# The pooling branch's sixteen evictions: half on VectorE, half on ScalarE, or all on ScalarE

## Chip, cores and metric

The kernel runs on one core of one Trainium2 chip. The metric is the time of one execution in microseconds (us), the median of the timed runs of the same program. A core has a matrix engine (TensorE, PE in the rows, with its weight loads as PEld), a vector engine (VectorE, DVE), an activation engine (ScalarE, ACT), GpSimd (POOL), and queues that start DMA transfers (SP's and POOL's among them). Each engine works through its own list of instructions in order and waits at semaphores for the others. Matmuls write to PSUM, which is read out ("evicted") by VectorE or ScalarE.

## What is computed

One decoder layer, in float32, for 512 prompt tokens and 8 x 4 sample tokens (T = 544 columns in all). Three token mixers run on the same input and are merged by gates, and a feed-forward part follows:

```
h      = x @ w_in
gates  = sigmoid(h[..., o3:] + b_gate)                  # three branches
p      = pool_branch(u_a)                               # windows 2/4/8/16, 4 groups of 64 channels
br_a   = einsum('btgc,gcd->btgd', p, pool_w) * pool_scale
br_b   = stick_breaking_attention(q, k, v) @ w_att_o
glu    = c_in[..., :256] * sigmoid(c_in[..., 256:])
br_c   = silu(layernorm(causal_depthwise_conv31(glu))) @ conv_pw
merged = gates[0] * br_a + gates[1] * br_b + gates[2] * br_c
x      = layernorm(ALPHA * x + merged @ w_out)
x      = layernorm(ALPHA * x + (silu(x @ wg) * (x @ wu)) @ wd)
```

The change lies in the line of `br_a`: the product of the pooled input `p` with `pool_w`, times `pool_scale`.

## The kernel before

Activations are held with channels on the 128 partitions and tokens along the columns, in two halves (`HALVES`): 288 columns (32 sample and 256 prompt tokens) and 256. Every large product is done in float32 from parts: an operand is split into a rounded high part and the rest (`split_psum`, lines 213 to 219, and `_Weights.prepare`, line 120, with a cast on ScalarE at line 134 and a difference on VectorE at line 135), and `gemm` (line 221) issues three matmuls for each pair of operands (line 229). A chunk of 128 output columns over the 1024 inputs is 24 matmuls for each half; its result lies in one of three PSUM banks (pool `mm`).

Around the change the program says, in this order: the pooling input (lines 354 to 387, ending in `ph_` and `pl_`, the two parts of `p`), the convolution's inputs (390 to 408), the pooling branch's product (503 to 518), two gates of the first branch (`gate0`, 522), and then the attention with its q, k and v chunks (`qkv_q`, `qkv_k`, `qkv_v`). The depthwise convolution's 31 taps for each of two channel blocks (`conv_work`, line 437, 60 instructions on VectorE after the first of each) are handed out late in the program (`pump`), but depend on early data alone.

The order that each engine gets is not the program's. The framework's planner runs a timeline of its own, takes the instructions that are ready, goes by their place in the program, and writes a fixed list for each engine. A tile from a pool with one buffer is handed out again when all readers of the one before are done, and a pool that is closed gives its memory to pools opened later, whose tiles wait for the old readers (`reuse_waits="tile"`).

The pooling product is eight blocks (two group pairs `gp`, two column tiles `m`, two halves). A block takes `pair()`, a tile `z` of two banks from a pool with one buffer, and fills both banks: two groups of 64 channels, one for each half of the array's rows, three matmuls each (line 512). Its two banks are multiplied by `pool_scale` on the way out to `mg`: bank 0 on ScalarE (line 518), bank 1 on VectorE (line 516). The same tile `z` is next used by the attention's first scores (`front`, line 582). The pools `s1` and `pp` (which holds `ph_` and `pl_`) are closed behind the blocks (519, 520); the attention's pool `att` is opened at line 612, and `qkv_q` copies its chunk out with line 218 on ScalarE (`qh`), line 219 on VectorE (`ql`), and line 535 on ScalarE (`qbd`). The gates' chunks are copied out at line 491 on ScalarE, passed through a sigmoid (494), and multiplied into `mg` on VectorE (500). The convolution's result is transposed at line 458.

Of the kernel before, what the change touches and what calls it, by code (L numbers as in the profile page):

```python
# [13 lines left out]
ALU = mybir.AluOpType  # L14
# [33 lines left out]
V_BG, V_PS, V_CB, V_CG, V_CLB, V_G1, V_B1, V_DW, V_SB, V_SR = 0, 24, 32, 34, 36, 38, 46, 54, 116, 124  # L48
# [101 lines left out]
def hybrid_layer_kernel(  # L150
# [6 lines left out]
    nc = tc.nc  # L157
# [13 lines left out]
    def bank(tag="mm"):  # L171
        return pst[tag].tile([P, 512], F32, tag=tag, name=tag)
# [4 lines left out]
    def pair():  # L177
        return pst["z"].tile([P, 2, 512], F32, tag="z", name="z")
# [58 lines left out]
    def vcol(c):  # L237
        return vt[:, c:c + 1]
# [15 lines left out]
    mg = mp_.tile([P, KD, T], F32, name="mg")  # L254
# [249 lines left out]
    for gp in range(2):  # L504
        for m in range(2):
            for hf, (c0, c1) in enumerate(HALVES):
                zz = pair()
                pss = [zz[:, s] for s in range(2)]
                for n_, (a, b) in enumerate(((pw[0], ph_), (pw[0], pl_), (pw[1], ph_))):
                    for s in range(2):  # L510
                        r = slice(64 * s, 64 * s + 64)
                        nc.tensor.matmul(pss[s][:, :c1 - c0], a[r, gp, m * P:(m + 1) * P], b[r, gp, c0:c1], start=n_ == 0, stop=n_ == 2)
                for s in range(2):
                    mo = 4 * gp + 2 * s + m
                    if s:
                        nc.vector.tensor_scalar(mg[:, mo, c0:c1], pss[s][:, :c1 - c0], vcol(V_PS + mo), None, op0=ALU.mult)  # L516
                    else:
                        nc.scalar.mul(mg[:, mo, c0:c1], pss[s][:, :c1 - c0], vcol(V_PS + mo))
    s1s.close()
    pps.close()  # L520
    late_constants()
# [205 lines left out]
    for b in range(DB):  # L727
# [11 lines left out]
        for br, g in [c for c, n_ in zip(steps, at_batch) if n_ == b]:  # L739
# [3 lines left out]
            elif br == 3:  # L743
                cw_ = w.next()
                for m in range(2):
                    mo = 2 * g + m
# [38 lines left out]
    for g in range(4):  # L785
# [7 lines left out]
        for m, hf in both:  # L793
                mo = 2 * g + m
                c0, c1 = HALVES[hf]
# [340 lines left out]
    for m in range(KD):  # L1136
        pss = [bank(), bank()]
# [52 lines left out]
    for m in range(KD - 1):  # L1190
        pss = [bank(), bank()]
# [140 lines left out]
```

## Time and profile before

| | us |
|---|---|
| median of three timed runs | 854.65 |
| lowest and highest of them | 854.51, 855.94 |
| the profiled execution | 858.24 |
| its span, first to last instruction | 854.5 |
| TensorE busy | 824.3 (96%) |
| VectorE busy | 570.0 (67%) |
| ScalarE busy | 409.8 (48%) |
| GpSimd busy | 175.8 (21%) |

The page gives busy times over the whole span; what one stretch is limited by is read from the windows of that stretch and from what TensorE waited for there. Starts of instructions are in us from the span's start. "mm" is a bank of the pool of that name, "z" the pair of banks, "mg" the branch's result, "acc" the convolution's sum, "wh" and "wl" the two parts of a weight chunk.

### The profile page before, as it was taken

The numbers are of one execution on the slowest core, as the hardware profiler recorded it, in microseconds if no ns is written. First come the engines' busy times: TensorE is split into PE (matmuls) and PEld (weight loads), VectorE is DVE, ScalarE is ACT, GpSimd is POOL, SyncE is SP. The second block draws the span as 40 slices with busy tenths as digits, with TensorE's granted clock in tenths as the row PEclk, the third lists the DMA queues.
The fourth block names the chain that finished last, engine by engine and source line by source line (L and its number), as shares of the span: only waits on it lengthen the run. The fifth ranks groups of instructions, "written<-read, shape, count | busy, mean of one in ns | idle before, by whom it ended". The sixth has DMA issues, their size and how long they took to land.

```text
span 854.5 us, 16236 instructions
## 1 busy us (share of the span) xinstructions
PE 824.3 (96%) x6707; PEld 778.4 (91%) x6707; DVE 570.0 (67%) x956; ACT 409.8 (48%) x703; POOL 175.8 (21%) x200
## 2 busy tenths in 40 slices
PE   8999799999999999999999999999999999999992
PEld 7998799888798878789998999999999999999992
DVE  4899956889545545459645898873338988842436
ACT  5434368787635433334415665552214655543231
POOL 1430000001627787310000322111000211110002
PEclk9999899999999999999998999999999999999997
DMA  9413132422727989774710134312335333213222
GB/s 297 133 35 108 55 89 84 125 66 65 278 90 238 364 290 351 250 253 149 198 51 1 43 91 115 98 35 69 102 108 137 106 103 102 78 50 87 82 85 104
DMA packets 119401, 110.34 MB, mean 129 GB/s; under 512 B 4897, under 2 KB 111233, under 8 KB 117153
## 3 DMA queue, kind: packets, MB, share of 16 engines
q1 hardware_dynamic: 110848, 73.12, 28.8%
q0 software_dynamic: 8480, 36.20, 12.0%
q8 instruction: 52, 0.85, 0.4%
q14 instruction: 21, 0.16, 0.1%
HBM read 104.44 MB, written 4.87 MB: 128 GB/s over the span
## 4 chain that ended last, share of the span: by engine, by line
PE 87%; DVE 7%; issue 2%; DMA 2%; ACT 1%; POOL 1%; SPq 0%; DVEq 0%; ACTq 0%
PE mm L229 77%; DVE acc L437 3%; PE z L678 2%; PE o L705 2%; PE z L582 1%; PE o L608 1%; PE tp L603 1%; DVE wl L135 1%; PE tp L820 1%; DMA vr<-in_cv,piv 1%; DMA xt<-in_x_t 1%; PE tp L897 0%; DVE mg L516 0%; DVE mg L500 0%; POOL mg L751 0%
## 5 line engine op out<-in xcount | busy, mean ns | idle before, releaser
L229 PE MATMUL mm<-xh,wh 128*128 128x256 f32 (+1 forms) x672 | 198.6, 296 | 2.6 <-DVE gt L493 0.9
L229 PE MATMUL mm<-xl,wh 128*128 128x256 f32 (+1 forms) x672 | 196.8, 293 | 0.5 <-DVE xl L216 0.4
L229 PE MATMUL mm<-xh,wl 128*128 128x288 f32 (+1 forms) x672 | 196.2, 293 | 0.2 <-DVE wl L135 0.2
L134 ACT CAST wh<-raw 128x1024 fp32r<-128x1024 f32 (+2 forms) x93 | 84.8, 915 | 158.0 <-PE mm L229 140.4
L135 DVE TENSOR_TENSOR wl<-raw,wh 128x1024 fp32r<-128x1024 f32 (+2 forms) x93 | 99.3, 1070 | 66.9 <-ACT wh L134 66.3
L229 PEld LDWEIGHTS mm<-xh,wh 128*128 128x128 f32 x672 | 128.2, 191 | 8.7 <-issue 3.8
L229 PEld LDWEIGHTS mm<-xl,wh 128*128 128x128 f32 x672 | 128.1, 191 | 4.6 <-issue 3.1
L229 PEld LDWEIGHTS mm<-xh,wl 128*128 128x128 f32 x672 | 127.9, 191 | 3.0 <-issue 2.2
L229 PE MATMUL mm<-gh,wh 128*128 128x288 f32 (+1 forms) x352 | 101.5, 290 | 0.0
L229 PE MATMUL mm<-gh,wl 128*128 128x288 f32 (+1 forms) x352 | 101.1, 288 | 0.0
L229 PE MATMUL mm<-gl,wh 128*128 128x288 f32 (+1 forms) x352 | 100.7, 287 | 0.0
L645 POOL DMA_INDIRECT kr<-in_ck,pix x64 | 67.0, 1047 | 35.8 <-issue 15.4
L229 PEld LDWEIGHTS mm<-gl,wh 128*128 128x128 f32 x352 | 66.3, 188 | 0.0
L229 PEld LDWEIGHTS mm<-gh,wl 128*128 128x128 f32 x352 | 66.1, 188 | 0.0
L990 POOL TENSOR_TENSOR gl<-sg,gh 128x272 fp32r<-128x272 f32 x24 | 22.9, 956 | 209.5 <-ACT gh L989 209.5
L229 PEld LDWEIGHTS mm<-gh,wh 128*128 128x128 f32 x352 | 65.9, 188 | 0.1
L990 POOL TENSOR_TENSOR gl<-g,gh 128x272 fp32r<-128x272 f32 x20 | 21.3, 1066 | 110.2 <-ACT gh L989 107.8
L437 DVE SCALAR_TENSOR_TENSOR acc<-ge,vt,acc 128x512 f32<-128x512 f32 x60 | 42.5, 749 | 0.1
L229 PE MATMUL mm<-mh,wh 128*128 128x256 f32 (+1 forms) x128 | 37.7, 294 | 0.0
L229 PE MATMUL mm<-ml,wh 128*128 128x256 f32 (+1 forms) x128 | 37.5, 293 | 0.0
L229 PE MATMUL mm<-mh,wl 128*128 128x256 f32 (+1 forms) x128 | 37.0, 289 | 0.0
L914 DVE TENSOR_TENSOR wl<-rawf,wh 128x1024 fp32r<-128x1024 f32 x22 | 27.3, 1242 | 9.6 <-ACT wh L913 9.5
(327 smaller groups left out, 2158.4 us busy)
## 6 DMA issues: line engine op xcount, KB each, us to landing
raw<-in_w_in SPq DMA_DIRECT2D x14, 1024.0 KB, 6.3
rawf<-in_w_g SPq DMA_DIRECT2D x22, 512.0 KB, 4.0
rawf<-in_w_u SPq DMA_DIRECT2D x22, 512.0 KB, 5.4
raw<-in_w_in SPq DMA_DIRECT2D x12, 512.0 KB, 3.9
raw<-in_w_d SPq DMA_DIRECT2D x16, 384.0 KB, 3.5
raw<-in_w_d SPq DMA_DIRECT2D x16, 320.0 KB, 3.3
raw<-in_w_out SPq DMA_DIRECT2D x4, 1024.0 KB, 5.5
raw<-in_w_att_o SPq DMA_DIRECT2D x4, 512.0 KB, 3.5
```

The source lines that it names most:

```text
L134: self.nc.scalar.copy(hi[:, a:b], v[:, a:b])
L135: self.nc.vector.tensor_tensor(out=lo[:, a:b], in0=v[:, a:b], in1=hi[:, a:b].bitcast(F32), op=ALU.subtract)
L229: ins = nc.tensor.matmul(ps[:, :n], lw, rr, start=first and s == 0, stop=last and s == len(steps) - 1, **kw)
L437: nc.vector.scalar_tensor_tensor(out=o, in0=v, scalar=dw, in1=o, op0=ALU.mult, op1=ALU.add)
L582: nc.tensor.matmul(zps[s][:, :wd], a[r, qs], b[r, :wd], start=n_ == 0, stop=n_ == 2)
L603: nc.tensor.transpose(tp[:, kb], rc[:, s, kb * P:(kb + 1) * P], ident)
L608: nc.tensor.matmul(op_[64 * s:64 * s + 64, :P], vtok[:, kb, 64 * s:64 * s + 64], ats[s][:, kb], start=kb == 0, stop=kb == i)
L645: nc.gpsimd.indirect_dma_start(out=kr[:, u].rearrange("p h c -> p (h c)"), out_offset=None, in_=ck, in_offset=bass.IndirectOffsetOnAxis(ap ...
L678: behind["z"] = nc.tensor.matmul(zp[32 * jj:32 * jj + 32, :256], qbd[:, hp, b], kvt[b, "k", jj][:, :, hp], start=hp == 0, stop=hp == 3)
L705: nc.tensor.matmul(op_[32 * c:32 * c + 32], at[:, j], kvt[b, "v", j // 4][:, j % 4], start=j >= 4, stop=False)
L914: nc.vector.tensor_tensor(out=l, in0=src, in1=h.bitcast(F32), op=ALU.subtract)
L990: nc.gpsimd.tensor_tensor(out=gl[:, f % NFC, c0:c0 + TH], in0=g, in1=gh[:, f % NFC, c0:c0 + TH].bitcast(F32), op=ALU.subtract)
```

## The change

The choice between the two engines goes away: both banks of a block are now evicted by ScalarE, one after the other, with the operation that it used for bank 0. Data, order in the program and matmuls are the same.

```
                 for s in range(2):
                     mo = 4 * gp + 2 * s + m
-                    if s:
-                        nc.vector.tensor_scalar(mg[:, mo, c0:c1], pss[s][:, :c1 - c0], vcol(V_PS + mo), None, op0=ALU.mult)
-                    else:
-                        nc.scalar.mul(mg[:, mo, c0:c1], pss[s][:, :c1 - c0], vcol(V_PS + mo))
+                    nc.scalar.mul(mg[:, mo, c0:c1], pss[s][:, :c1 - c0], vcol(V_PS + mo))
```

## Rows read from the trace of the kernel before

**Rows 1.** Windows: length, busy us by engine, granted clock, DMA share, GB/s.

```profile
45.00:84.00 39.00, 37.95 (x304) 35.85 (x302) 38.96 (x56) 15.85 (x24) 6.00 (x7) 1.00 0.25 72
84.00:91.00 7.00, 1.46 (x15) 1.05 (x14) 7.00 (x13) 2.73 (x6) 0.00 (x0) 0.82 0.26 75
91.00:96.00 5.00, 4.81 (x25) 4.62 (x26) 5.00 (x9) 0.78 (x3) 0.21 (x1) 0.56 0.00 0
103.00:123.00 20.00, 20.00 (x162) 19.43 (x162) 11.05 (x20) 12.68 (x26) 1.32 (x2) 1.00 0.33 97
234.00:239.00 5.00, 4.06 (x23) 3.87 (x20) 2.68 (x7) 0.67 (x2) 0.00 (x0) 0.66 0.38 151
```

**Rows 2.** Instructions of line 512: duration min/median/max in ns, first and last start.

```profile
L512 PE MATMUL z<-ph,wh x16: 381/390/398, 45.1 to 85.9; 64*128 64x288 f32 x8, 64*128 64x256 f32 x8
```

**Rows 3.** Timeline, ScalarE: start us, duration us, operation, [idle before <- releaser].

```profile
80.80 1.06 ACT L134 CAST wh<-raw 128x1024 fp32r<-128x1024 f32 x1 [2.38 <-PE mm L229]
84.68 0.50 ACT L518 ACTIVATE mg<-z,vt 128x288 f32<-128x288 f32 x1 [2.82 <-PE z L512]
86.41 1.04 ACT L134 CAST wh<-raw 128x1024 fp32r<-128x1024 f32 x1 [1.23 <-PE z L512]
87.37 0.47 ACT L518 ACTIVATE mg<-z,vt 128x256 f32<-128x256 f32 x1
87.73 0.65 ACT L218 ACTIVATE qh<-mm 128x256 fp32r<-128x256 f32 x2
...
91.02 0.40 ACT L535 ACTIVATE qbd<-mm 64x32 f32<-64x32 f32 x2 [2.38 <-DVE ql L219]
```

**Rows 4.** Timeline, VectorE, same columns.

```profile
85.31 0.50 DVE L516 TENSOR_SCALAR mg<-z,vt 128x288 f32<-128x288 f32 x1
85.74 2.72 DVE L437 SCALAR_TENSOR_TENSOR acc<-ge,vt,acc 128x512 f32<-128x512 f32 x4
...
90.19 0.47 DVE L516 TENSOR_SCALAR mg<-z,vt 128x256 f32<-128x256 f32 x1
90.58 0.40 DVE L219 SCALAR_TENSOR_TENSOR ql<-mm,qh 128x256 fp32r<-128x256 f32 x1
```

**Rows 5.** Timeline, TensorE, same columns.

```profile
77.92 0.28 PE L229 MATMUL mm<-xh,wh 128*128 128x256 f32 x1
...
84.35 0.29 PE L512 MATMUL z<-ph,wl 64*128 64x288 f32 x2
85.87 0.39 PE L512 MATMUL z<-ph,wh 64*128 64x256 f32 x2 [1.23 <-DVE mg L516]
...
90.80 0.47 PE L582 MATMUL z<-kh,qh 64*128 64x128 f32 x2 [4.31 <-DVE mg L516]
91.47 0.58 PE L229 MATMUL mm<-xh,wh 128*128 128x256 f32 x1 [0.19 <-ACT qbd L535]
...
95.43 0.28 PE L229 MATMUL mm<-xh,wh 128*128 128x256 f32 x1
95.55 0.28 PE L229 MATMUL mm<-xl,wh 128*128 128x256 f32 x1
```

**Rows 6.** Groups by line, 40:112: xcount | busy us, mean ns | idle before.

```profile
L516 DVE TENSOR_SCALAR mg<-z,vt 128x288 f32<-128x288 f32 (+1 forms) x8 | 3.9, 485 | 0.0
L518 ACT ACTIVATE mg<-z,vt 128x288 f32<-128x288 f32 (+1 forms) x8 | 3.9, 485 | 2.8 <-PE z L512 2.8
```

**Rows 7.** TensorE's waits, 40 to 112 us: total us, times, longest us.

```profile
PE z L512 <- DVE mg L516: 1.7, 2, 1.2
PE mm L229 <- ACT gt L491: 0.6, 1, 0.6
```

**Rows 8.** Window of one us around 88 us, columns as in group 1.

```profile
88.00:89.00 1.00, 0.00 (x0) 0.00 (x0) 1.00 (x2) 0.64 (x3) 0.00 (x0) 0.77 0.00 0
```

**Rows 9.** Chain of waits around the convolution's first transposes: start us, us, what.

```profile
122.83 0.44 PE tp L458 x4
```

## The prediction, made before the change was run

> **What bounds the kernel now.** I read the windows by stage first, then TensorE's waits, then the rows of the four engines around the place where the change sits. TensorE is the bound: from 45 to 84 us it is busy 37.95 of 39 us, and from 103 to 123 us all 20 [rows 1]. The one early hole is 84 to 91 us: TensorE busy 1.46 of 7 us, VectorE busy all 7, and in 91 to 96 us the granted clock is 0.56 [rows 1]. So a change there is worth what of this hole it closes; VectorE's 8 evictions matter only as what TensorE waits for. In the 45 to 84 us window VectorE is busy 38.96 of 39 us and ScalarE 15.85 [rows 1].
>
> The hole comes about thus. The sixteen evictions belong to eight blocks of six matmuls (L512). All blocks go through one pair of banks, tile z, with one buffer: block n+1 cannot start before both evictions of block n are done. The blocks begin at 45.1 us and the last at 85.9 us [rows 2], (85.9 - 45.1)/7 = 5.8 us apart, though a block is only some 0.7 us of matmul. ScalarE's half of a pair is quick. VectorE's half stands in a full queue: for block 7 it begins 0.63 us after ScalarE's (85.31 against 84.68), for block 8 2.8 us after (90.19 against 87.37) [rows 3, 4]. In all eight pairs VectorE's begins later; 0.63 us is the smallest lag.
>
> The head pair's q columns follow. Their first half is finished in PSUM at 77.9 us [rows 5], ScalarE has 2.82 us idle before 84.68, yet it copies qh out only at 87.73, behind block 8's eviction [rows 3]. By the code that is a wait for memory: the pool att takes the space of ph and pl, which block 8 is the last to read. The trace shows the order, not the reason. With q and the first half of k unread, the three banks of mm are full, and TensorE stands: 1.23 us before block 8, then 4.31 us until VectorE's eviction at 90.19 frees z for the first scores (L582) [rows 4, 5].
>
> **The change part by part.** Removed from VectorE: eight L516, mean 485 ns alone [rows 6]; in a full queue the start of one to the start of the next instruction is 0.39 us (90.19 to 90.58) or 0.43 us (85.31 to 85.74) [rows 4], so 4 x 0.43 + 4 x 0.39 = 3.3 us. Alone, this moves VectorE's later work 3.3 us forward.
>
> Added to ScalarE: eight more L518, mean 485 ns, the same as VectorE's [rows 6]; behind another one the next starts 0.36 us later (87.37 to 87.73) [rows 3]. The second of a pair ends 0.36 us after the first, and 0.36 is under the smallest lag of 0.63 us. In sum 8 x 0.36 to 0.485 = 2.9 to 3.9 us on an engine with 23 of 39 us idle: I cost it at nothing, covered by that idle time; without that cover it is 3.9 us at most and never a gain. No wait of a new kind comes in. The second eviction waits for its block's last matmul, like the one ahead of it. Queued behind the pair are the weight casts (L134), the gate evictions (L491) and qh, and TensorE waits for the last two. A table load is not added, since the operation is that of the eight before. No DMA moves, and SP's and POOL's queues are not passed.
>
> One page speaks against the change. "TensorEngine Tiling (Array Packing)" of the Trainium skill, section "PSUM Bottleneck", says to use both ScalarE and VectorE for emptying PSUM. By that, a block's eviction would get 0.36 us longer; the rows say that it gets shorter in all eight, since VectorE is late by 0.63 us or more.
>
> What the hole is worth, by its own stretches:
> - 69 to 71 us: two waits, 0.5 us for L516 (1.7 less the 1.23) and 0.6 us for a gate's tile [rows 7], which waits for VectorE too: 1.1 us.
> - 84 to 91 us: 7 - 1.46 = 5.54 us [rows 1].
> - 91.47 to 95.43 us: 18 steps of matmul take 3.96 us, 0.22 us each, where the next takes 0.12 us (95.43 to 95.55) [rows 5]. That is the half clock, 1.2 GHz; it fell within 88 to 89 us (mean 0.77) after some 2 us without matmul [rows 8]. At the full 2.4 GHz, 18 x 0.117 = 2.1 us: 1.85 us to be had, and 0.2 us for the wait at 91.47.
>
> Sum 1.1 + 5.54 + 1.85 + 0.2 = 8.7 us. It is all to be had only if block 8 is through before q wants its memory at 77.9 us, so if a block takes no more than (77.9 - 45.1)/7 = 4.7 us in place of 5.8. A block's own time 0.7 us, two evictions 0.36 + 0.49, and a cast of 1.05 us in front of them (86.41, 1.04 us [rows 3]) make 2.6 us. The rest of a block's interval is where the planner puts it among the gate matmuls, which no row prices: between 0 and the 3.2 us that are left of today's 5.8. I take 2.0 us, since the planner can start a block from the moment z comes free, and so expect the last block to begin by 45.1 + 7 x 4.6 = 77.3 us or sooner.
>
> What is late next: VectorE's queue. If TensorE comes 8.7 us earlier and VectorE 3.3 us, VectorE trails by 5.4 us more than now. The taps need be done only for the first transposes of the convolution at 122.83 us [rows 9], and VectorE idles 20 - 11.05 = 8.95 us between 103 and 123 us [rows 1], so as a sum it fits. But ql (90.58 us, then qbd at 91.02 [rows 3, 4]) and the first scores stand in that queue, and each can make TensorE wait. Bounds: 0, if the idle time lies right, and the whole 5.4 us, if it does not. I take 2.2 us, nearest to the 1.23 us wait of block 8 with one more of its kind. Behind 123 us TensorE is nearly always busy, so an earlier TensorE carries through.
>
> Gain 8.7 - 2.2 = 6.5 us. The profiled execution took 858.24 us, 854.5 of it the span; the three timed runs have a median of 854.65 us. The gain is taken off either: 851.7 us for a profiled one, **848.2 us** for the median.
>
> **The rivals.**
> - The hole only shortens. The planner leaves the order of TensorE as it is, with blocks 7 and 8 behind k. Then block 7 is evicted at 84.68 + 0.36 + 0.50 = 85.54 in place of 85.81, block 8 ends 0.3 us earlier, the cast and two evictions run to 88.0, qh and kh to 89.1, and scores and second half of k come 1.8 us earlier; with the 1.1 us at 69 us that is 2.9 us, the clock still falling: 851.8 us. For: ScalarE's order around qh may stem from the planner and not from memory. Against: the planner places by when z is free.
> - VectorE is the bound. TensorE gains only what VectorE sheds, 3.3 us: 851.3 us. For: VectorE busy 38.96 of 39 us. Against: its idle time from 103 us on.
> - Given back later. The planner orders the rest anew, and a gap such as the one of 0.94 us that took the clock to a mean of 0.66 in 234 to 239 us [rows 1] (5 x 0.34 x 2 / 2 = 1.7 us) comes three or four times more: near 854.6 us, no change.
> - Slower. The taps that now run under the hole are put in front of ql, kl and the first scores, and three banks run dry three times as long as z did today for block 8: 3 x 3.7 us (86.5 to 90.19), with one more fall of the clock, 1.85 us: 13 us lost against 8.7 us won, 858.9 us. It decides once the new waits up to 123 us exceed 8.7 us. For: taps are always ready and fill VectorE. Against: the 8.95 us idle.
> - The page's rule, by a mechanism of this kernel: were VectorE prompt, serial evictions would hold z 0.36 us longer for eight blocks, 2.9 us: 857.5 us. The smallest lag of 0.63 us leaves it 2 in 100.
>
> **How the numbers follow.** Forecast 0.54 (its own range 846 to 851 us); hole shortened or VectorE the bound, 0.16 together; given back 0.13; slower by the taps 0.15; serial evictions 0.02. A measurement of this kernel tells some 0.2%, 1.7 us, from no change. Faster: 0.54 + 0.16 = 0.70; same 0.13; slower 0.15 + 0.02 = 0.17. The low end, 845 us, is the whole 8.7 us and part of one of the later falls of the clock; the high end, 856 us, takes in no change and the lesser losses. Left out: about 0.04 below and 0.12 above.
>
> **What would show it.** Right: no L516 on VectorE; the sixteen L518 in pairs 0.36 us apart; the last L512 before some 78 us; qh out right behind q's matmuls; no TensorE wait over 1 us and a granted clock of 1.00 from 84 to 96 us. Wrong: the last L512 still behind k's first half; TensorE waiting for ql, kl or zt behind taps; scores that begin earlier with convolution transposes no earlier; or a longer stretch behind 200 us.

## The result, and the profile after

The changed kernel takes 845.38 us (median of five runs, 843.94 to 849.24) beside 854.69 us (median of five) for the kernel before; the ratio is 0.9879, with a 95% interval of 0.9847 to 0.991. By the medians it is 9.3 us faster, by the ratio 10.3 us (7.7 to 13.1), where 6.5 us were forecast. Side by side it was run three times more, with ratios of 0.9906 (0.9874 to 0.9939), 0.9897 (0.9834 to 0.9961) and 0.9926 (0.9895 to 0.9956). In three of the five groups of runs below the kernel before took 874 to 880 us and not 855, and in the traces of these groups the excess lies behind 200 us; so a kernel's time is compared with that of the kernel before in its own group, and the stretch of the change by its own length.

The profiled execution took 845.32 us, its span 843.5 us. In the windows around the change (length, busy us of TensorE, its weight loads, VectorE, ScalarE, GpSimd, then granted clock) the hole of [rows 1] is gone:

```profile
45.00:84.00 39.00, 39.00 (x313) 36.62 (x312) 38.93 (x54) 21.52 (x37) 6.59 (x7) 1.00 0.29 85
84.00:91.00 7.00, 7.00 (x58) 6.83 (x57) 6.46 (x11) 2.56 (x7) 0.97 (x1) 1.00 0.03 7
91.00:96.00 5.00, 5.00 (x44) 4.92 (x44) 4.58 (x10) 3.06 (x8) 0.54 (x1) 1.00 0.51 161
84.00:123.00 39.00, 39.00 (x315) 37.55 (x316) 34.55 (x62) 23.12 (x49) 3.06 (x5) 1.00 0.29 84
```

TensorE is busy without a gap from 45 to 123 us, at a clock of 1.00. ScalarE's share of the first stretch went from 15.85 to 21.52 of 39 us; VectorE is still full there, with no eviction of the product in it. The instructions of the blocks and of the evictions (minimum, median and maximum in ns, first and last start; then count, busy us and mean ns) answer to [rows 2] and [rows 6]:

```profile
L512 PE MATMUL z<-ph,wh x16: 381/390/398, 45.7 to 75.8; 64*128 64x288 f32 x8, 64*128 64x256 f32 x8
```

```profile
L515 ACT ACTIVATE mg<-z,vt 128x288 f32<-128x288 f32 (+1 forms) x16 | 6.9, 486 | 3.7 <-PE z L512 3.6
```

The blocks are (75.8 - 45.7)/7 = 4.3 us apart in place of 5.8. The last one begins 3.3 us before q's first half is finished at 78.79 + 0.29 = 79.08 us, with this matmul:

```profile
78.79 0.29 PE L229 MATMUL mm<-xh,wl 128*128 128x288 f32 x1
```

Sixteen evictions on ScalarE take 486 ns each. ScalarE's and VectorE's timelines (start us, duration us, operation, idle before and releaser) answer to [rows 3, 4]:

```profile
77.35 0.84 ACT L515 ACTIVATE mg<-z,vt 128x256 f32<-128x256 f32 x2
78.07 1.12 ACT L494 ACTIVATE gt<-gt 128x1088 f32<-128x1088 f32 x1
79.21 1.28 ACT L293 ACT_TABLE_LOAD   x1
80.50 0.39 ACT L218 ACTIVATE qh<-mm 128x256 fp32r<-128x256 f32 x1
81.92 0.38 ACT L218 ACTIVATE qh<-mm 128x256 fp32r<-128x256 f32 x1 [1.03 <-PE mm L229]
```

```profile
82.80 0.73 DVE L219 SCALAR_TENSOR_TENSOR ql<-mm,qh 128x256 fp32r<-128x256 f32 x2
...
85.92 0.41 DVE L216 TENSOR_TENSOR kl<-mm,kh 128x256 fp32r<-128x256 f32 x1
```

Block 8's pair leaves at 77.35 us, and behind a sigmoid and a table load qh follows at 80.50, 7.2 us sooner than before; ql follows at 82.80. From 40 to 112 us the table of TensorE's waits is empty, where [rows 7] stood. The three longest waits of TensorE behind 112 us (total us, times, longest):

```profile
PE tp L894 <- DVE y L886: 1.5, 1, 1.5
PE mm L229 <- DVE gt L493: 0.9, 1, 0.9
PE o L605 <- ACT at L601: 0.7, 1, 0.7
```

To measure the stretch alone I take the time from the first block's first matmul to the first product of the new keys (line 663 before, 660 after), where both kernels have done the same work: 221.1 - 45.1 = 176.0 us before, 212.8 - 45.7 = 167.1 us after, **8.9 us less**.

```profile
L663 PE MATMUL z<-qbd,ksf x8: 379/379/403, 221.1 to 222.7; 128*32 128x256 f32 x8
```

```profile
L660 PE MATMUL z<-qbd,ksf x8: 379/379/403, 212.8 to 214.4; 128*32 128x256 f32 x8
```

The two profiled spans differ by 11.0 us. Behind the new keys the changed kernel takes another 2.7 us less (854.5 - 221.1 = 633.4 us against 843.5 - 212.8 = 630.7 us), and its first block begins 0.6 us later. The section on the prediction shows what of the 2.7 us is the clock.

### The profile page after: what moved, and what is told of

The parts are those of the page before. It is cut to its first block, busy times and chain, and to the rows that moved or that the text cites. A ratio compares the mean times of both kernels' runs of the same rounds, so it can differ in the third digit from the quotient of the medians.

```text
span 843.5 us, 16236 instructions
## 1 busy us (share of the span) xinstructions
PE 819.7 (97%) x6707; PEld 773.2 (92%) x6707; DVE 568.2 (67%) x948; ACT 413.2 (49%) x711; POOL 177.3 (21%) x200
## 4 chain that ended last, share of the span: by engine, by line
PE 93%; DMA 2%; DVE 2%; ACT 1%; issue 1%; POOL 1%; SPq 0%; DVEq 0%; POOLq 0%; ACTq 0%
PE mm L229 83%; PE z L675 2%; PE o L702 2%; PE z L579 1%; PE o L605 1%; PE tp L600 1%; PE tp L817 1%; DMA vr<-in_cv,piv 1%; DMA xt<-in_x_t 1%; PE z L512 1%; PE tp L894 0%; PE o L705 0%; POOL mg L748 0%; ACT xf L895 0%; POOL kr L642 0%
## 5 line engine op out<-in xcount | busy, mean ns | idle before, releaser
L135 DVE TENSOR_TENSOR wl<-raw,wh 128x1024 fp32r<-128x1024 f32 (+2 forms) x93 | 101.2, 1091 | 67.3 <-ACT wh L134 66.7
L229 PEld LDWEIGHTS mm<-xh,wh 128*128 128x128 f32 x672 | 126.5, 188 | 8.7 <-issue 4.0
L229 PEld LDWEIGHTS mm<-xl,wh 128*128 128x128 f32 x672 | 126.2, 188 | 4.5 <-issue 3.1
L229 PEld LDWEIGHTS mm<-xh,wl 128*128 128x128 f32 x672 | 126.2, 188 | 3.3 <-issue 2.4
```

Source lines behind the costliest of these rows:

```text
L135: self.nc.vector.tensor_tensor(out=lo[:, a:b], in0=v[:, a:b], in1=hi[:, a:b].bitcast(F32), op=ALU.subtract)
L229: ins = nc.tensor.matmul(ps[:, :n], lw, rr, start=first and s == 0, stop=last and s == len(steps) - 1, **kw)
```

## The experiments

Two theories were set against each other. The pace theory: the time is set by when z comes free; that places block 8 in TensorE's list before or behind q and k, and block 8 holds the memory that q's copies wait for. The relief theory: VectorE is full, and the gain is what it sheds. The table gives the stretch (first block to new keys) and the time against the kernel before in the same group. The kernel before has one trace. Two traces of the same program differ by up to 1.4 us in the stretch (e2 and e10), so a difference of 2 us there is not far from that.

| kernel | stretch, us | ratio (95%) |
|---|---|---|
| before | 176.0 | 1 |
| changed (e8, e15, e18) | 167.4, 167.1, 167.1 | 0.9906, 0.9897, 0.9926 |
| all sixteen on VectorE (e1, e9) | 174.1, 173.0 | 0.996 (0.9926 to 0.9994), 0.9969 (0.9947 to 0.9991) |
| blocks 1 to 4 on ScalarE (e2, e10) | 173.9, 172.5 | 0.9974 (0.9946 to 1.0002), 0.9956 (0.9925 to 0.9987) |
| blocks 5 to 8 on ScalarE (e3, e11) | 174.2, 173.8 | 0.9935 (0.9913 to 0.9956), 0.9929 (0.9901 to 0.9958) |
| changed, VectorE's load back (e4, e12) | 167.1, 167.1 | 0.9979 (0.9949 to 1.001), 0.9901 (0.9866 to 0.9935) |
| changed, three times that load (e13) | 173.9 | 1.0022 (0.9985 to 1.0059) |
| before, ph and pl in memory of their own (e5) | 169.3 | 0.992 (0.9889 to 0.9952) |
| changed, the same (e6) | 167.1 | 0.9889 (0.9844 to 0.9934) |
| before, taps held back (e7) | 185.8 | 1.0094 (1.0062 to 1.0127) |

The time follows the stretch to within 3 us, except in e3 and e11 (by the ratio 5.7 and 6.2 us faster, by the stretch 1.8 and 2.2), e4 (1.8 against 8.9) and e13 (1.9 us slower against 2.1 us faster). By the traced executions these differences lie outside the stretch, and no run here explains them; what follows is told by the stretch.

**All on one engine, the other one.**

```
-                    if s:
-                        nc.vector.tensor_scalar(mg[:, mo, c0:c1], ...)
-                    else:
-                        nc.scalar.mul(mg[:, mo, c0:c1], ...)
+                    nc.vector.tensor_scalar(mg[:, mo, c0:c1], ...)
```

> All sixteen evictions on VectorE, none on ScalarE. Pace theory (the time is set by when tile z comes free, and so where the planner puts block 8 in TensorE's list): z is freed by VectorE's queue as before, the list has block 8 behind the first half of k again, so the hole at 84 to 91 us stays and the pair's second half adds some 0.4 us to it: 855 to 856 us. Relief theory (the gain is the 3.3 us of work that VectorE sheds): VectorE gets 3.3 us more in a stretch where it is always busy: 858 us.

> All sixteen evictions on VectorE again, since the kernel before took 879 us on the chip of the first four and not 855. There the stretch of 84 to 96 us still had a hole (TensorE busy 7.71 of 12 us, clock 0.72). Pace theory: block 8 starts some 2 us earlier than in the kernel before and the hole shrinks but stays: 852 to 855 us. Relief theory: 3.3 us slower than before, 858 us.

Before e1 both theories expected the kernel before or worse; it was 2 to 3 us shorter in the stretch and 0.3 to 0.4% faster in time, and e9 repeated it. VectorE had some 3.3 us more to do, so a relief cannot be what made this gain. The hole stayed, smaller (TensorE busy 2.71 of 7 us in e9, before 1.46), and was now TensorE waiting for kh and for qbd (total us, times, longest):

```profile
PE mm L229 <- ACT qbd L532: 2.4, 1, 2.4
PE z L579 <- ACT kh L215: 1.8, 1, 1.8
```

**Half of the blocks.**

```
-                    if s:
+                    if s and gp == 1:        # e2, e10; gp == 0 in e3, e11
```

> Both evictions on ScalarE for blocks 1 to 4 only; blocks 5 to 8 split as before. Pace theory: blocks 2 to 5 come closer together, but block 8 still stands behind the first half of k in TensorE's list, so the hole at 84 to 91 us and its half clock stay and only the 1.1 us of waits near 70 us can go: 853 to 854.5 us. Relief theory: half of 3.3 us, with the measured gain shared evenly half of 9.3 us: 850 to 853 us.

> ScalarE alone for blocks 1 to 4, again. Pace theory: block 8 behind the first half of k, hole and half clock stay, 852 to 854.5 us. Relief theory: half the gain, 850 us.

> Both evictions on ScalarE for blocks 5 to 8 only; blocks 1 to 4 split as before. Pace theory: block 8 is still behind the first half of k in TensorE's list, but z is freed by ScalarE some 1.8 us sooner; the hole is shorter and the clock falls all the same or just escapes: 851 to 853 us. Relief theory: half, 850 to 853 us, with no difference from blocks 1 to 4.

> ScalarE alone for blocks 5 to 8, again. Pace theory: the hole is shorter by some 2 us and the clock falls all the same, 851 to 853 us. Relief theory: half the gain, 850 us, the same as for blocks 1 to 4.

Half of the blocks gave 1.8 to 3.5 us of the 8.9 in the stretch, whichever half it was. By the time alone e3 and e11 would fit the relief theory's half as well or better (5.7 and 6.2 us); it is the traces that tell the two theories apart here. In e10 block 8 stood behind the first half of k as before, began at 83.5 us, and TensorE waited for its eviction on VectorE with the clock falling again (the wait, then the windows as above):

```profile
PE z L582 <- DVE mg L516: 2.6, 1, 2.6
```

```profile
84.00:91.00 7.00, 3.36 (x17) 3.00 (x16) 7.00 (x13) 3.02 (x8) 0.21 (x1) 0.78 0.25 72
91.00:96.00 5.00, 5.00 (x40) 5.00 (x40) 5.00 (x8) 1.32 (x3) 0.00 (x0) 0.97 0.00 0
```

So the gain in the stretch is not shared out by blocks: the hole closes when block 8 is not left behind q and k, and 4.3 us a block do that while a mix does not (last blocks at 83.5 to 85.7 us). e3 and e11 are the rival "the hole only shortens" in the flesh: they keep the waits near 70 us, so its price is 1.8 us without the 1.1, and 1.8 and 2.2 us were measured in the stretch. That e10 won more than the 1.1 us of the waits near 70 us was not expected; its block 8 began at 83.5 us, before at 85.9.

**VectorE's load given back, once and three times.** To the changed kernel this adds instructions on VectorE that take the maximum of a piece of mg with itself; z is freed by ScalarE alone as before.

```
                     nc.scalar.mul(mg[:, mo, c0:c1], pss[s][:, :c1 - c0], vcol(V_PS + mo))
+                    if s:
+                        for _ in range(3):   # e13; once in e4, e12
+                            nc.vector.scalar_tensor_tensor(out=mg[:, mo, c0:c1], in0=mg[:, mo, c0:c1], scalar=1.0, in1=mg[:, mo, c0:c1], op0=ALU.mult, op1=ALU.max)
```

> The changed kernel with eight instructions added on VectorE (each takes the maximum of a piece of mg with itself, some 0.4 us), so that VectorE has its old load back while z is still freed by ScalarE alone. Pace theory: block 8 stays ahead of q in TensorE's list and the time stays that of the changed kernel, 845.4 us, within 1.5 us. Relief theory: the 3.3 us come back, 848.7 us or more.

> The changed kernel with eight instructions of some 0.4 us on VectorE, again. On the chip of the first four there was no hole from 45 to 123 us. Pace theory: 846 us within 2 us, or up to 2 us more if VectorE, which now trails by the whole 8.7 us, makes TensorE wait behind 123 us. Relief theory: 849 us or more, with waits for VectorE already between 84 and 123 us.

The added instructions (count, busy us, mean ns) and the windows in e12:

```profile
L517 DVE SCALAR_TENSOR_TENSOR mg<-mg 128x288 f32<-128x288 f32 (+1 forms) x8 | 3.4, 431 | 0.0
```

```profile
45.00:84.00 39.00, 39.00 (x313) 36.62 (x312) 38.93 (x59) 21.65 (x37) 6.91 (x7) 1.00 0.29 85
84.00:91.00 7.00, 7.00 (x58) 7.00 (x57) 6.63 (x11) 2.44 (x7) 0.97 (x1) 1.00 0.02 5
91.00:96.00 5.00, 5.00 (x44) 4.75 (x43) 4.58 (x11) 2.77 (x6) 0.54 (x1) 1.00 0.51 161
```

With 3.4 us of the shed work back on VectorE the stretch is 167.1 us in both runs, to the tenth the changed kernel's, and TensorE has no gap from 45 to 96 us. The relief theory falls for the stretch. In e12 the whole gain is there in the time too (0.9901); in e4, the same program, most of it was given back behind 200 us, where TensorE waited in many places (busy 113.82 of 130 us from 200 to 330 us, 117.79 in e12). As the two have one order, the order alone does not make that difference; its cause is open.

> The changed kernel with 24 such instructions on VectorE, three to a block, some 9 us of work in all. From its first block to the first product of the new keys the changed kernel takes 167.1 us, and with eight of them also 167.1 us; VectorE idles about 4.5 us between 84 and 123 us of the changed kernel. If VectorE has slack in this stage only by its idle time: 6 to 9 us more than it has are asked of it, TensorE waits for it and the stretch grows by 2 to 5 us. If the planner only moves the taps behind what TensorE needs, and the convolution's transposes go later with other work in front: 167 to 168 us still, and no new wait over 0.6 us before 123 us.

TensorE's waits from 100 to 213 us (total us, times, longest), and the window behind 123 us:

```profile
PE tp L603 <- ACT at L604: 1.8, 1, 1.8
PE tp L603 <- ACT cf L472: 0.8, 1, 0.8
PE z L582 <- DVE zt L584: 0.6, 1, 0.6
```

```profile
123.00:213.00 90.00, 86.72 (x691) 77.07 (x690) 71.40 (x138) 65.62 (x131) 8.38 (x14) 0.94 0.25 77
```

Three times the load, 9.9 us (9.0 of it from 45 to 84 us), made the stretch 6.8 us longer: TensorE now waited, not in the old place but behind 140 us, in the attention and behind the convolution's norm, 90 - 86.72 = 3.3 us in all, and the clock fell (a mean of 0.94 there, where the changed kernel has 1.00). Two of the three waits end with ScalarE's work; that VectorE's queue is behind them follows from the edit alone. So VectorE's slack in the stretch lies between the 3.4 us of e12, which cost nothing, and 9.9 us. Of the two expectations the first was nearer, with its 2 to 5 us too small.

**The memory.** ph and pl become parts of oh, which nothing writes before the attention's first output; the attention's pool then takes over no memory from them.

```
-    ph_ = pp.tile([P, 2, T], F32R, name="ph")
-    pl_ = pp.tile([P, 2, T], F32R, name="pl")
+    ph_, pl_ = oh[:, 0:2], oh[:, 2:4]
```

> The kernel before, split evictions as they were, but ph and pl lie in oh, which is not written until the attention's first output, in place of a pool whose memory the attention's tiles take over. Memory theory: q's copies no longer wait for block 8, so the banks of mm come free, TensorE goes on with q, k, v and gates while the blocks trickle through, and most of the 7.5 us around 84 to 96 us goes although z is as slow as before: 846 to 849 us. If the planner's order alone put qh behind block 8: no change, 854.7 us.

The blocks' matmuls with their first and last start, the windows, and ScalarE's first copy of q:

```profile
L511 PE MATMUL z<-oh,wh x32: 273/338/405, 46.8 to 91.9; 64*128 64x288 f32 x16, 64*128 64x256 f32 x16
```

```profile
84.00:91.00 7.00, 7.00 (x58) 6.67 (x57) 6.48 (x11) 2.68 (x6) 0.66 (x1) 1.00 0.27 77
91.00:96.00 5.00, 5.00 (x43) 4.70 (x42) 5.00 (x9) 1.98 (x4) 0.54 (x1) 1.00 0.10 28
```

```profile
80.02 0.38 ACT L218 ACTIVATE qh<-mm 128x256 fp32r<-128x256 f32 x1
```

Here VectorE evicts its half as before, and the last block's matmuls begin at 91.9 us, later than before; yet TensorE has no hole, since qh is copied out at 80.02 us, ahead of the last blocks. The stretch is 6.7 us shorter. What the trace of before showed as an order was a wait for memory. The change and this edit cure the same thing from its two ends, as the two together show:

> The changed kernel with ph and pl in oh. Memory theory: block 8 is through before q asks for the memory, so nothing is left to gain: 845.4 us, within 1.5 us. If memory still held something up in the changed kernel, 843 us or less.

167.1 us, and 0.9889: nothing is added. The 2.2 us between e5 and the changed kernel contain the two waits near 70 us, which e5 still has (TensorE 37.90 of 39 us from 45 to 84 us).

**The queue of taps.**

```
+                    with tc.issue_after(hold.ins):   # hold: the last eviction
-                    nc.vector.scalar_tensor_tensor(out=o, in0=v, scalar=dw, in1=o, op0=ALU.mult, op1=ALU.add)
+                        nc.vector.scalar_tensor_tensor(out=o, in0=v, scalar=dw, in1=o, op0=ALU.mult, op1=ALU.add)
...
-                        nc.vector.tensor_scalar(mg[:, mo, c0:c1], ...)
+                        hold = nc.vector.tensor_scalar(mg[:, mo, c0:c1], ...)
```

> The kernel before, split evictions, with the convolution's taps held back on VectorE behind its last eviction of the product, so that VectorE's half finds a short queue. If the queue of taps is what makes VectorE's half late: z comes free within 1 to 2 us of each block, block 8 is through well before 78 us, and the hole at 84 to 91 us is gone; 40 us of taps then start some 25 us later and the convolution's transposes with them, which TensorE may have to wait for: 846 to 851 us. If VectorE's half is late for another reason (the weight differences of 1.2 us, the order of the two engines): the hole stays and the late taps come on top, 856 us or more.

VectorE's evictions (line 517 there) and one of ScalarE's, then the windows, then TensorE's waits:

```profile
54.66 0.48 DVE L517 TENSOR_SCALAR mg<-z,vt 128x256 f32<-128x256 f32 x1 [1.55 <-ACT mg L519]
...
59.21 0.52 DVE L517 TENSOR_SCALAR mg<-z,vt 128x288 f32<-128x288 f32 x1 [1.85 <-ACT mg L519]
...
68.38 0.52 DVE L517 TENSOR_SCALAR mg<-z,vt 128x288 f32<-128x288 f32 x1 [2.37 <-ACT mg L519]
...
72.88 0.48 DVE L517 TENSOR_SCALAR mg<-z,vt 128x256 f32<-128x256 f32 x1 [1.25 <-ACT mg L519]
```

```profile
54.15 0.47 ACT L519 ACTIVATE mg<-z,vt 128x256 f32<-128x256 f32 x1 [2.04 <-PE z L513]
```

```profile
45.00:84.00 39.00, 39.00 (x316) 36.65 (x315) 17.43 (x25) 17.80 (x29) 5.55 (x8) 1.00 0.24 73
84.00:91.00 7.00, 6.95 (x54) 6.51 (x53) 7.00 (x13) 2.85 (x7) 0.00 (x0) 1.00 0.25 75
```

```profile
PE tp L472 <- DVE cna L466: 4.1, 1, 4.1
PE tp L459 <- DVE acc L438: 2.0, 2, 1.8
```

With the taps away VectorE is idle before four of its eight evictions and the hole is gone (6.95 of 7 us), so it was the queue of taps that made VectorE's half late enough to matter. That block 8 would be through well before 78 us did not come true: the blocks are 4.8 us apart (47.5 to 81.4 us), and the last begins 1.3 us behind the end of q's first half (79.78 + 0.29 us):

```profile
79.78 0.29 PE L229 MATMUL mm<-xh,wl 128*128 128x288 f32 x1
...
81.40 0.39 PE L513 MATMUL z<-ph,wh 64*128 64x256 f32 x2
```

So block 8 need not be ahead of q, as the prediction asked; a little behind it cost nothing. But 40 us of taps that start after 80 us are late for the convolution's transposes and norm (4.1 and 2.0 us of waits, and a clock of 0.91 from 123 to 213 us), and the kernel is 0.9% slower where 4 to 9 us faster was expected: the taps have to run in that stretch.

**The changed kernel again**, in each later group:

> The changed kernel again, beside the three above on the same chip: 845.4 us, with a spread of some 2 us between runs, as the clock falls or not after the short waits behind 200 us.

> The changed kernel beside the other two on the same chip: 167.1 us from the first block to the new keys, and 0.990 of the kernel before.

> The changed kernel beside the two, for the same chip: 0.990 of the kernel before.

It came out at 847.16, 871.18 and 849.16 us (beside 856.28, 879.66 and 855.02 us), with the stretch at 167.1 to 167.4 us each time.

**The same for the gates.** The evictions of line 493 move to ScalarE: 32 of them, of the second and third branch (not 36, as the first expectation says), and in e17 the last four as well.

```
-                if br == 0 and g < GACT:
+                if br or g < GACT:             # e14, e16; always in e17
```

> The changed kernel with the evictions of all other gates (line 493) moved from VectorE to ScalarE too, 36 of them. In the changed kernel TensorE waits 0.9 us for one of them near 225 us and once or twice 0.7 us beside it. If what held for the product's evictions holds here (the engine with the shorter queue frees the bank sooner): 0.5 to 1.5 us faster than the changed kernel, 844 to 846 us. If ScalarE, whose sigmoids, exponentials and table loads stand in the same queue there, frees the banks later: 1 to 4 us slower, 847 to 850 us.

> The changed kernel with the gates of the second and third branch evicted by ScalarE too (32 instructions of line 493; the four of the first branch's fourth gate stay on VectorE), again. On the last chip, where the kernel before took 879.7 us, it was 863.2 us beside 871.2 us for the changed kernel. On a chip where the kernel before takes 855 us the waits that it takes away are 0.9 us for a gate and some of 0.7 us: 843 to 845 us beside 846.

> The same with the four evictions of the first branch's fourth gate moved as well, so that no gate is evicted by VectorE. If every eviction moved to the shorter queue helps: the 0.3 us that TensorE still waited for line 493 goes, the time as with 32 or up to 0.5 us less. If the order planned anew decides: any difference within 2 us.

Each stands beside the changed kernel in its own group: e14 had 0.9828 (0.9773 to 0.9884) against 0.9897 (0.9834 to 0.9961), e16 and e17 had 0.9928 (0.9904 to 0.9951) and 0.9904 (0.9873 to 0.9935) against 0.9926 (0.9895 to 0.9956). The intervals overlap each time: no difference that these runs can tell. The wait for line 493 went from 0.9 us (e18) to 0.3 us in e16, and to none in e17, but the wait for page data grew from 0.4 us (e18) to 2.4 and 1.7 us (total us, times, longest, in e17):

```profile
PE o L702 <- DMA vr<-in_cv,piv: 1.7, 1, 1.7
```

So it is no sure improvement on the changed kernel.

## Why the prediction was right in kind and too small

- **What bounds it, and the hole.** Right. The memory that block 8 holds, told from the code alone, is now shown by e5, and VectorE's late half and its queue by e7. The three full banks and the fall of the clock were not tried by themselves; they went with the hole in e5, e7 and the changed kernel. That block 8 must be through before q is finished is stricter than e7 shows.
- **The worth of the hole, 8.7 us.** Right: the stretch got 8.9 us shorter.
- **The block's interval.** At most 4.6 us was forecast, 4.3 us came; the last block at 75.8 us where 77.3 or sooner was forecast.
- **ScalarE at nothing.** Right: 5.7 us more busy time from 45 to 84 us and no wait of TensorE for it before 112 us.
- **New waits for VectorE, 2.2 us.** This is the step that failed: they were 0. I took them from the wait of block 8, though that wait came of VectorE's late half of z, which the change removes. The rows had the answer: the idle 8.95 us from 103 to 123 us cover the 5.4 us by which VectorE trails. From 84 to 123 us VectorE idled 39 - 29.53 = 9.47 us before and 39 - 34.55 = 4.45 us after, so 5.0 us were taken up there:

```profile
84.00:123.00 39.00, 33.27 (x256) 31.82 (x255) 29.53 (x50) 18.96 (x39) 2.07 (x4) 0.91 0.28 83
```

  That TensorE did not wait for ql and kl on the way is measured; that the planner sees to it by putting them ahead of taps is argued, not shown. e13 shows that the worry was real: with 9.9 us of further work waits do come, and the stretch is 6.8 us longer. Without the 2.2 us the forecast would have been 854.65 - 8.7 = 845.95 us.
- **What lies behind 200 us.** The ratio of 0.9879 is 10.3 us of 854.69 us, so 844.4 us, just below the low end of 845 us, where the forecast had the whole 8.7 us and a part of one later fall of the clock. What the stretch leaves of it is 1.4 us. The falls differ between executions of one program: at the last norm of the first part TensorE waits 1.5 us (the L894 wait above, L897 before) in all three profiles that follow, and the clock over 8 us from there had a mean of 0.57 in the profile before, 0.79 in that of the changed kernel, and 1.00 in e8, the changed kernel again (same columns; before, changed, e8):

```profile
460.00:468.00 8.00, 6.60 (x31) 6.31 (x32) 5.23 (x10) 6.08 (x11) 0.00 (x0) 0.57 0.01 2
```

```profile
450.00:458.00 8.00, 6.89 (x39) 6.32 (x40) 4.88 (x7) 5.83 (x12) 0.00 (x0) 0.79 0.01 2
```

```profile
450.00:458.00 8.00, 6.59 (x48) 6.02 (x49) 5.12 (x9) 7.29 (x14) 0.00 (x0) 1.00 0.01 2
```

  By these means the slow clock cost 8 x 0.43 = 3.4 us in the profile before and 8 x 0.21 = 1.7 us in that of the changed kernel (estimates). The fall in 234 to 239 us of [rows 1], 1.7 us by the prediction, did not come in the profile after, nor in e8, after the same wait for line 493 (0.9 us, above). Together that is 3.4 us, against the 2.7 us that the profiles differ by behind the stretch. A term of some 1 to 2 us either way belonged into the range for that.
- **The rivals.** "The hole only shortens" is e11, not the change. "VectorE is the bound" falls by the stretch of e12. "Given back later" did not come with the change; in e4 it did, for a cause that is open. "Slower by the taps" has its mechanism in e13 and e7, and needed 9.9 us of extra work or the taps moved. For the Trainium skill's rule, see the last section: the two halves never ran at the same time before (smallest lag 0.63 us, an eviction 0.51 us at most), so nothing was lost by putting them on one engine.

## What to carry to other kernels

Where one small buffer is handed round a loop, look at who frees it last and how long that engine's queue is, and not at the cost of the eviction: here the second of two engines of equal speed began 0.6 to 4.0 us behind the first. Follow what the loop's end holds (here memory that a later stage waits for), since most of the gain comes in one piece when the loop's end is no longer far behind that point; half of the edit gave a fifth to two fifths of it in the stretch. And before a new wait is charged to an engine that will trail, count its idle time in the stretch where it can catch up.

## What the runs showed that was not expected

VectorE's half of a pair waits for ScalarE's half. In e7, where VectorE has less to do, its eviction is released by ScalarE's all four times that it idles before one, and begins 0.04 us after that one's end (54.15 + 0.47 = 54.62 us, then 54.66 us). In the kernel before all eight begin behind the end of ScalarE's, block 1's 4.0 us after its start, block 7's 0.63 us [rows 3, 4]; there VectorE also has its taps to finish, so these rows alone do not show the wait:

```profile
46.39 0.50 ACT L518 ACTIVATE mg<-z,vt 128x288 f32<-128x288 f32 x1
```

```profile
50.41 0.51 DVE L516 TENSOR_SCALAR mg<-z,vt 128x288 f32<-128x288 f32 x1
```

The program has them on two banks with no data between them, but they share the tile z that they read and the tile mg that they write; which of the two makes the order was not tried. So a split over the engines cost a handover and saved nothing, and the rival of a prompt VectorE that runs beside ScalarE could not have come true in this kernel. That may also be a reason for all sixteen on VectorE being 2 to 3 us shorter in the stretch than the split, though that was not tried by itself.

"TensorEngine Tiling (Array Packing)" of the Trainium skill, section "PSUM Bottleneck", asks for both engines when PSUM is emptied. The runs here don't bear it out for two halves of one tile: one engine alone, either of them, was faster than both (ratios of 0.9879 to 0.9926 for ScalarE, 0.996 and 0.9969 for VectorE). A split without the wait between the halves was not run.
